# One hybrid mixer block on one core: the mixers' steps handed out in another order

## The chip, the cores and the metric

The kernel runs on 1 core of one Trainium2 chip. The metric is the device time of one execution in microseconds (us), the median of several runs. TensorE (PE in the profile) multiplies matrices and transposes, VectorE (DVE) and ScalarE (ACT) do the elementwise work, GpSimd (POOL) a few small operations, and SyncE (SP) issues most of the transfers. Each engine works through its own queue of instructions in order.

## What is computed

The reference is one block with a latent stream `x` of 1024 tokens by 1024 channels and a context of 256 tokens. One input projection feeds four mixers of 256 channels each, their outputs are joined and projected back, and a feed-forward part follows:

```python
y_a, yc_a = mlstm_mixer(z[..., :OFF_B], zc_a, ...)           # bidirectional chunkwise mLSTM
y_b = sgu_mixer(z[..., OFF_B:OFF_C], ...)                    # spatial gating, chunks of 128
y_c = conv_mixer(z[..., OFF_C:OFF_D], ...)                   # 31 taps, LayerNorm, SiLU
y_d, yc_d = s5_mixer(z[..., OFF_D:], zc_d, ...)              # bidirectional S5
y = jnp.concatenate([y_a, y_b, y_c, y_d], axis=-1) @ w_out[l]
x = layer_norm(ALPHA * x + g1 * y, ln1_w[l], ln1_b[l])
x = layer_norm(ALPHA * x + g2 * swiglu(x * (1.0 + sc2) + sh2, w_ffn_in[l], w_ffn_out[l]), ln2_w[l], ln2_b[l])
```

`g1`, `sh2`, `sc2` and `g2` are parts of the modulation `silu(c) @ w_mod + b_mod`, which is 6 times 1024 columns wide.

## The kernel before

Large products are three passes over values split in a high and a low half (`split2`: the high half on ACT, L831, the low on DVE, L832). Weights come in pieces of 512 KB through two `raw` buffers on SP's queue and are split into `whl` or `pg` tiles. `projT` (L861) makes a projection with channels on the partitions, `projK` (L870) with tokens on them. A projection `latT` writes its result with an activation (L1084).

Two forces set the order. The code says in which order steps are handed to a list scheduler: what comes first in the code goes first, and a later step fills in where an earlier one is not ready. Buffers and PSUM banks then hold a step back until an earlier user has let go. PSUM has three banks `mm` for the projections, two `a`, two `b` and one `c`. Bank `c` is shared by the modulation (L1010), the gating's mixing (L611, L647) and both transposes of the convolution's norm (L691, L700).

The steps of the mixers, and the lines to which they go:

- mLSTM (`y["a"]`): `mlstm_gates` (L370 to L474), `mlstm_states` (L478 to L525: the recurrent states `mC` of all eight chunks, a chain of small steps), then `mlstm_chunk` for each of 8 chunks of 128 tokens. A chunk has PE make the scores in bank `a` (L536) and, for each of two directions, the decay exponents in bank `b` (L543, L544, L546). ACT takes the exponential into `mD` (L549), DVE multiplies the scores on (L553), PE makes the states' part (L559) and the chunk's own part (L568), and DVE puts them together (L563 to L579). `mlstm_norm` takes two chunks at a time (L589 to L603).
- Gating (`y["b"]`): two projections `u` and `v`, the latter into `gv` (L870 and L1142), constants of the mixing weights (L611), and for each half of the tokens a norm (L636) and the mixing (`sgu_mix`: PE L647 into bank `c`, DVE L650 and L653).
- Convolution (`y["c"]`, in place in `ap`): `conv_taps` for each of two blocks of channels (50 DVE operations each, L673 to L681), and `conv_norm` for each of four quarters of the tokens (PE L691 into `c`, DVE L623 to L627, ACT L625 and L696, PE L700 into `c` again, and ACT's SiLU L702).
- Modulation: six late groups of 512 columns (`mod_late`). A group loads 8 pieces of 256 KB (`mw`, in two buffers) on SP's queue. DVE adds each onto the one buffer `macc` (L997, L999), PE sums over the partitions (L1010), and DVE adds the offsets (L1011). The first two groups make `g1`, spread over a tile by PE at L1151; the third is half of `sh2`.

`out_proj(0)` follows. For a half of the tokens it splits the four mixers' outputs (ACT L1198, DVE L1199), loads `x` (L1202) and multiplies by `w_out` (L1211), eight row blocks in the order d, b, c, a:

```python
KORD = (6, 7, 2, 3, 4, 5, 0, 1)
```

Three of its tiles stand in the three `mm` banks at a time, with 24 matmuls each: 6 with d, 6 with b, 6 with c, 6 with a. L1215 and L1216 add the result to `x`; `ln1` norms it (L1231 transposes it for the feed-forward part).

ACT holds the tables of one set of functions at a time: exponential (L549), square root (L625) and SiLU (L702) each bring a row `ACT_TABLE_LOAD` when the set before was another.

In the words of the new order's table, the code before hands out: `ctx_k ctx_v conv_in.0 conv_in.1 conv_w val gates key states query chunk.0 chunk.1 chunk.2 chunk.3 out_gate norm.0 norm.2 mod.0 mod.1 mod.2 sgu_u sgu_v gate1 sgu_w sgu.0 taps.0 taps.1 conv_n.0 conv_n.1 chunk.4 chunk.5 chunk.6 chunk.7 norm.4 norm.6 sgu.1 conv_n.2 conv_n.3`.

Of the kernel before, what the change touches and what calls it, by code (L numbers as in the profile page):

```python
# [705 lines left out]
D = 1024  # L706
# [54 lines left out]
    return np.ascontiguousarray(np.concatenate([c[n] for n, _ in CST], 1))  # L761


def body(tc, A, out):
# [5 lines left out]
    with st:  # L770
# [272 lines left out]
        Wk = [wtile(A["wk"][kh], 4, 256) for kh in range(2)]
        for j in range(2):
            ps = ps_mm()
            projK(Wk, ctxl(j), ps[:, 0:256])
            a.activation(kxc[:, j], ps[:, 0:256], AF.Copy, scale=0.125)
        Wv = wvg()
        for j in range(2):
            ps = ps_mm()  # L1050
            projK(Wv, ctxl(j), ps[:, 0:272])
            evac_vg(ps, vxc[:, j], j)
# [14 lines left out]
        wc = mx.tile([128, 2, 31], F32, name="wc")  # L1067
        gp.dma_start(wc, A["conv_t"])
        tc.keep_in_program_order(v.tensor_scalar(wc, wc, 0.5, None, op0=MUL))
        wcs = mx.tile([128, 2, 16], F32, name="wcs")  # L1070
        conv_sums(e, wc, wcs)

        vx = mx.tile([128, 8, 4, 65], F32, name="vx", tag="vx")
        Wv = wvg()
        for j in range(8):
            ps = ps_mm()
            projK(Wv, lat(j), ps[:, 0:272])
            evac_vg(ps, vx[:, j], 2 + j)
# [17 lines left out]
        kT = latT(page([128, 2, 1024]), "k", AF.Copy, scale=0.125)
        C = mp.tile([128, 8, 2, 2, 65], F32, name="mC", tag="mC")
        mlstm_states(e, G, kxc, vxc, kT, vx, C, mp)
        qT = latT(page2([128, 2, 1024]), "q", AF.Copy)
        y["c"] = ap.rearrange("p j r t -> p j (r t)")[:, :, 0:D]  # L1100
        hb = C.rearrange("p c r d x -> p c (r d) x")[:, :, :, 0:64]

        def chunks(hf):
            for c in range(hf * 4, hf * 4 + 4):
                mlstm_chunk(e, G, c, qT, kT, vx[:, c], hb[:, c], mp)

        def norms(hf):
            for c in range(hf * 4, hf * 4 + 4, 2):
                mlstm_norm(e, hb[:, c:c + 2], mp.tile([128, 8, 64], F32, name="msq", tag="mD", bufs=3), c, col["mnw"],
                           y["a"], y["a"], mp, NC=2)  # L1110

        def mlstm_half(hf):
            chunks(hf)
            norms(hf)

        def conv_half(hf):
            for q in range(hf * 2, hf * 2 + 2):
                conv_norm(e, ap, y["c"], q, col["clw"], col["clb"], mx)
# [16 lines left out]
        y["b"] = latT(page2([128, 2, 1024]), "u", AF.Gelu_apprx_tanh)  # L1135
        gv = page2([128, 8, 256])
        Wb = [wtile(A["wb"][kh], 4, 256) for kh in range(2)]
        for j2 in range(4):
            ps = ps_mm()
            for i in range(2):  # L1140
                projK(Wb, lat(j2 * 2 + i), ps[:, i * 256:(i + 1) * 256])
            a.activation(gv[:, j2 * 2:j2 * 2 + 2].rearrange("p i x -> p (i x)"), ps, AF.Gelu_apprx_tanh)  # L1142

        g1d = page([128, 2, D])
        g1 = g1d[:, 1]
        for i in range(8):
            v.tensor_scalar(g1d[:, 0, i * 128:(i + 1) * 128], e.ident, m2c[:, i:i + 1], None, op0=MUL)
        for c in range(2):
            cs_ = slice(c * 512, (c + 1) * 512)
            ps = ps_mm()  # L1150
            pe.matmul(ps, lhsT=bc(e.one, [128, 128]), rhs=g1d[:, 0, cs_], start=True, stop=True)  # L1151
            a.copy(g1[:, cs_], ps)
        wsT, bsb = mp.tile([128, 4, 128], F32, name="gw"), mp.tile([128, 2, 128], F32, name="gbs", tag="mC0")
        gp.dma_start(wsT, A["sgu_wt"])
        gp.dma_start(bsb, A["sgu_bb"])
        B = bsb
        sgu_consts(e, col["glb"], bsb, wsT, B)
# [442 lines left out]
```

## Time and profile before

| | us |
|---|---|
| median of 3 runs (lowest, highest) | 1175.17 (1174.21, 1177.67) |
| the profiled execution | 1174.72 |
| its span, first to last instruction | 1172.9 |
| PE busy | 1130.4 |
| DVE busy | 915.1 |
| ACT busy | 477.3 |
| mean granted clock of PE, full speed as 1 | 0.982 |

A row of the profile gives the engine, the line of the code, the operation, the tile written and the tiles read (`out<-in`), and a count. The chain of waits runs back from the last instruction, at each step to what released it. A row of the timeline has start, duration, instruction, and in brackets the idle time before it with what ended it. A matmul on 32-bit floats that are not split (L536, L559, L568, L611, L647, L691, L1010) counts as two records in the trace and one in an order listing. `PEclk` is the clock granted to PE.

### The profile page before, as it was taken

How to read it: one execution, taken by the hardware profiler on the slowest of the kernel's cores; microseconds unless marked ns; L12 is line 12 of the kernel's file. 1: busy time of each engine (PE TensorE's matmuls, PEld its weight loads, DVE VectorE, ACT ScalarE, POOL GpSimd, SP SyncE). 2: the span in 40 equal slices, each digit the busy share in tenths (PEclk: the TensorE clock that was granted, in tenths of full speed). 3: DMA queues.
4: the chain of work that ended last, by engine and by line, in shares of the span. 5: the costliest groups of instructions: out<-in, count | busy, mean ns of one | idle time of the engine just before them, and what ended most of it. 6: DMA issues, size and time to landing. Idle time of an engine off the chain costs nothing.

```text
span 1172.9 us, 15466 instructions
## 1 busy us (share of the span) xinstructions
PE 1130.4 (96%) x5763; PEld 909.8 (78%) x5763; DVE 915.1 (78%) x1751; ACT 477.3 (41%) x746; POOL 10.6 (1%) x33
## 2 busy tenths in 40 slices
PE   7989999999999899999999999999999989999996
PEld 4777788668897687768887888888887778888884
DVE  7778899988996699879868677776778767766775
ACT  4735444412428464582233332333232336433431
POOL 0010000000000000000000000000000000000000
PEclk8999999999999799999999999999999999999998
DMA  9652101121233165452233544435444789766621
GB/s 349 233 176 75 49 24 52 45 86 37 81 118 125 55 203 193 114 209 79 101 138 113 180 182 177 152 135 202 178 169 170 270 269 321 242 200 214 195 101 72
DMA packets 68316, 178.41 MB, mean 152 GB/s; under 512 B 7761, under 2 KB 15089, under 8 KB 66834
## 3 DMA queue, kind: packets, MB, share of 16 engines
q1 hardware_dynamic: 67826, 176.45, 43.8%
q0 software_dynamic: 272, 0.70, 0.3%
q8 instruction: 45, 0.74, 0.3%
q10 hardware_dynamic: 144, 0.29, 0.1%
q14 instruction: 29, 0.24, 0.1%
HBM read 136.80 MB, written 40.62 MB: 151 GB/s over the span
## 4 chain that ended last, share of the span: by engine, by line
PE 72%; DVE 14%; DMA 6%; ACT 5%; issue 2%; DVEq 0%; SPq 0%; ACTq 0%
PE mm L1372 16%; PE mm L861 11%; PE a L1372 8%; PE mm L1497 5%; PE mm L1211 4%; PE b L1372 4%; PE b L861 4%; PE a L1497 3%; PE b L1497 3%; PE mm L870 2%; PE c L1497 2%; DVE whl L832 2%; DVE pg L832 1%; PE b L568 1%; DMA mw<-in_w_mod_dram 1%
## 5 line engine op out<-in xcount | busy, mean ns | idle before, releaser
L861 PE MATMUL mm<-pg,whl 128*128 128x512 f32 x792 | 218.2, 410 | 1.9 <-ACT pg L1234 1.2
L831 ACT CAST whl<-raw 128x512 fp32r<-128x512 f32 (+1 forms) x198 | 119.6, 621 | 238.0 <-PE mm L1372 51.2
L1372 PE MATMUL mm<-pg,whl 128*128 128x512 f32 x864 | 206.0, 390 | 0.4 <-DVE whl L832 0.3
L1372 PEld LDWEIGHTS mm<-pg,whl 128*128 128x128 f32 x864 | 161.9, 188 | 35.6 <-issue 0.7
L861 PEld LDWEIGHTS mm<-pg,whl 128*128 128x128 f32 x792 | 144.2, 192 | 36.9 <-issue 5.6
L832 DVE TENSOR_TENSOR whl<-raw,whl 128x512 fp32r<-128x512 f32 (+1 forms) x198 | 133.1, 689 | 50.0 <-ACT whl L831 48.1
L1372 PE MATMUL a<-pg,whl 128*128 128x512 f32 x432 | 104.7, 390 | 3.7 <-ACT whl L831 3.7
L1372 PEld LDWEIGHTS a<-pg,whl 128*128 128x128 f32 x432 | 80.7, 188 | 21.4 <-ACT whl L831 4.9
L832 DVE TENSOR_TENSOR pg<-raw,pg 128x1024 fp32r<-128x1024 f32 (+1 forms) x52 | 59.6, 1150 | 23.3 <-ACT pg L831 23.2
L832 DVE TENSOR_TENSOR pg<-whl,pg 128x1024 fp32r<-128x1024 f32 (+1 forms) x42 | 47.4, 1133 | 32.4 <-ACT pg L831 28.4
L831 ACT CAST pg<-raw 128x1024 fp32r<-128x1024 f32 (+1 forms) x52 | 51.5, 991 | 50.4 <-DMA raw<-in_w_dram 18.7
L831 ACT CAST pg<-whl 128x1024 fp32r<-128x1024 f32 (+1 forms) x42 | 41.1, 980 | 66.4 <-PE c L1497 25.4
L870 PE MATMUL mm<-whl,pg 128*128 128x256 f32 (+1 forms) x448 | 64.9, 292 | 0.7 <-ACT whl L831 0.7
L870 PEld LDWEIGHTS mm<-whl,pg 128*128 128x128 f32 x448 | 59.3, 193 | 3.2 <-issue 1.7
L1372 PE MATMUL b<-pg,whl 128*128 128x512 f32 x216 | 51.9, 389 | 0.0
L1211 PE MATMUL mm<-whl,pg 128*128 128x512 f32 x192 | 49.9, 397 | 1.0 <-DVE pg L1199 1.0
L1211 PE MATMUL mm<-pg 128*128 128x512 f32 x192 | 49.5, 399 | 0.0
L1497 PE MATMUL mm<-pg,pg 128*128 128x512 f32 x171 | 48.0, 389 | 0.0
L1497 PE MATMUL a<-pg,pg 128*128 128x512 f32 x162 | 47.2, 390 | 0.3 <-DVE hs L1511 0.3
L1497 PE MATMUL b<-pg,pg 128*128 128x512 f32 x162 | 47.1, 389 | 0.0
L1372 PEld LDWEIGHTS b<-pg,whl 128*128 128x128 f32 x216 | 40.5, 188 | 8.4
L1211 PEld LDWEIGHTS mm<-whl,pg 128*128 128x128 f32 x192 | 35.3, 188 | 9.3 <-DVE pg L1199 1.8
(473 smaller groups left out, 1880.8 us busy)
## 6 DMA issues: line engine op xcount, KB each, us to landing
raw<-in_w_dram SPq DMA_DIRECT2D x59, 512.0 KB
gd<-pg SPq DMA_DIRECT2D x22, 1024.0 KB
whl<-gd SPq DMA_DIRECT2D x35, 512.0 KB
pg<-in_w2k_dram SPq DMA_DIRECT2D x11, 1024.0 KB
td<-pg SPq DMA_DIRECT2D x11, 1024.0 KB
raw<-td SPq DMA_DIRECT2D x20, 512.0 KB
raw<-in_wo_dram SPq DMA_DIRECT2D x16, 512.0 KB
raw<-in_wt_dram SPq DMA_DIRECT2D x14, 512.0 KB
```

What stands on the lines that cost most here:

```text
L568: pe.matmul(ps[:, x * 65:(x + 1) * 65], lhsT=D[d][:, x], rhs=vx[:, h, :], start=True, stop=True)
L831: a.copy(hi, r)
L832: v.tensor_tensor(lo, r, hi.bitcast(F32), op=SUB)
L861: pe.matmul(ps[h], lhsT=W(wi, k), rhs=rhs(hi, h, k), **f)
L870: pe.matmul(ps, lhsT=lhs(hi, k), rhs=Ws[k // 4](wi, k % 4), start=(k == 0 and n == 0), stop=(k == 7 and n == 2))
L1211: pe.matmul(ps, lhsT=Yr(hi, half, k)[:, t * 128:(t + 1) * 128], rhs=Ws[k // 2](wi, k % 2), start=(i + n == 0), stop=(i == 7 and n == 2))
L1372: pe.matmul(ps, lhsT=W[:, wi, k, :], rhs=B[b][hi][:, k], start=(first and k + n == 0), stop=(k == 3 and n == 2), skip_group_check=True)
L1497: pe.matmul(ps[t], lhsT=Ag[:, hi, k, t * 128:(t + 1) * 128], rhs=Bg[:, wi, k], start=(first and k0 + k + m == 0), stop=(k0 + k == NK - 1 a ...
```

## The change

The block of the mixers, from the context's projections to the mixers' last norms, is cut into named steps. Each step has the same instructions as before. A string gives the order in which they are handed to the scheduler. `sgu.1`, `conv_n.2` and `conv_n.3`, which stood just ahead of `out_proj(0)`, are among them.

```diff
+ORDER = """ctx_v ctx_k conv_in.1 conv_in.0 conv_w val gates key taps.0 states query chunk.3 taps.1 out_gate chunk.0 mod.2 chunk.2
+conv_n.0 chunk.1 sgu_u norm.2 mod.0 mod.1 norm.0 sgu_v gate1 sgu_w sgu.0 chunk.7 chunk.4 chunk.6 conv_n.1 chunk.5 conv_n.2
+norm.4 norm.6 sgu.1 conv_n.3"""
...
+        @do
+        def states():
+            C = mp.tile([128, 8, 2, 2, 65], F32, name="mC", tag="mC")
+            mlstm_states(e, X.G, kxc, vxc, X.kT, X.vx, C, mp)
+            X.hb = C.rearrange("p c r d x -> p c (r d) x")[:, :, :, 0:64]
...
+        def chunk(c):
+            mlstm_chunk(e, X.G, c, X.qT, X.kT, X.vx[:, c], X.hb[:, c], mp)
...
+        def mod(i):
+            mod_late(range(i, i + 1), lambda: mx.tile([128, 512], F32, name="macc", tag="kxc"),
+                     lambda: mx.tile([128, 512], F32, name="mw", tag=("vxc", "mw")[next(mq) % 2]), "c")
...
+        def conv_n(q):
+            conv_norm(e, ap, y["c"], q, col["clw"], col["clb"], mx)
+
+        def run(order):
+            for n in order.split():
+                if n in step:
+                    step[n]()
+                else:
+                    f, i = n.rsplit(".", 1)
+                    dict(conv_in=conv_in, chunk=chunk, norm=norm, mod=mod, sgu=sgu_half, taps=taps, conv_n=conv_n)[f](int(i))
+
+        run(ORDER)
...
-        chunks(0)
-        y["a"] = latT(page2([128, 2, 1024]), "o", AF.Sigmoid)
-        norms(0)
-        mq = iter(range(99))
-        mod_late(range(0, 3), lambda: mx.tile([128, 512], F32, name="macc", tag="kxc"),
-                 lambda: mx.tile([128, 512], F32, name="mw", tag=("vxc", "mw")[next(mq) % 2]), "c")
...
-        sgu_half(0)
-        taps(0)
-        taps(1)
-        conv_half(0)
-        mlstm_half(1)
...
-        sgu_half(1)
-        conv_half(1)
         out_proj(0)
```

In the new file the lines below 764 keep their numbers; L831 and L861 become L836 and L866, L870 becomes L875, L1010 becomes L1015, L1198 becomes L1245, and L1211 becomes L1258.

**ACT, the second half's chunks.** First the program of before, where ACT serves chunks 4 to 7 (exponentials into `mD`) and the convolution's first two norms (`cmv`, `cxn`, `ap`):

```order
L549 ACT_TABLE_LOAD
L549 ACTIVATE mD<-b 128x512
L625 ACT_TABLE_LOAD
L625 ACTIVATE cmv<-cmv,oz 128x2
L696 ACTIVATE cxn<-c,cmv 128x256 x2
L549 ACT_TABLE_LOAD
L549 ACTIVATE mD<-b 128x512
L702 ACT_TABLE_LOAD
L702 ACTIVATE ap<-c,cols 128x256 x2
L549 ACT_TABLE_LOAD
L549 ACTIVATE mD<-b 128x512
L1198 CAST pg<-ap 128x1024
```

The same place in the changed program, up to the split of the same `ap`:

```order
L625 ACT_TABLE_LOAD
L625 ACTIVATE cmv<-cmv,oz 128x2
L549 ACT_TABLE_LOAD
L549 ACTIVATE mD<-b 128x512
L836 CAST pg<-raw 128x1024
L549 ACTIVATE mD<-b 128x512
L696 ACTIVATE cxn<-c,cmv 128x256 x2
L549 ACTIVATE mD<-b 128x512 x2
L702 ACT_TABLE_LOAD
L702 ACTIVATE ap<-c,cols 128x256 x2
L1245 CAST pg<-ap 128x1024
```

The exponentials now stand together, and one SiLU (of quarter 1) instead of two stands in this place; quarter 0's norm is done earlier.

**PE, the same place.** Before, from the last matmuls with b to the first with c (`mm<-pg` alone, without `whl`); `gw` is the gating's mixing weight, `cst` the identity, `cr` the constants of the decay:

```order
L700 MATMUL c<-cst,cxn 128x128 x4
L568 MATMUL b<-vx,mD 128x65 x4
L647 MATMUL c<-gw,pg_3292 64x128 x11
L559 MATMUL a<-mC,pg_2600 128x130 x4
L568 MATMUL b<-vx,mD 128x65 x4
L536 MATMUL a<-pg_2600,pg 128x128 x4
L647 MATMUL c<-gw,pg_3292 64x128 x5
L1211 MATMUL mm<-pg 128x512 x3
```

And in the changed program, again up to the first matmuls with c. Ahead of these rows stand three transposes L700, three matmuls L1258 with b and four L568:

```order
L1258 MATMUL mm<-whl,pg 128x512
L559 MATMUL a<-mC,pg_2652 128x130 x4
L568 MATMUL b<-vx,mD 128x65 x4
L536 MATMUL a<-pg_2652,pg 128x128 x4
L543 MATMUL b<-cr 128x512
L544 MATMUL b<-mR_2264,cr 128x512
L546 MATMUL b<-cr,mAL_2263 128x512
L543 MATMUL b<-cr 128x512
L544 MATMUL b<-mR_2275,cr 128x512
L546 MATMUL b<-cr,mAL_2274 128x512
L691 MATMUL c<-cst,ap 64x128 x8
L1258 MATMUL mm<-pg 128x512 x18
```

The mixing L647 of the second half has left this place. The last matmul with b now stands one chunk ahead of those with c, which follow 18 in a row.

**PE, the modulation.** Before, the three late groups lie in the projections of the gate and of the gating, one after the other:

```order
L1010 MATMUL c<-oz,macc 128x1 x4
L861 MATMUL mm<-pg,whl 128x512 x8
L600 MATMUL b<-cst,msq 128x128 x4
L861 MATMUL mm<-pg,whl 128x512 x13
L870 MATMUL mm<-whl,pg 128x256 x79
L1010 MATMUL c<-oz,macc 128x1 x4
L870 MATMUL mm<-whl,pg 128x256 x113
L1151 MATMUL mm<-pg,oz 128x512 x2
```

These are the second and the third group. In the changed program the second and third handed out (`mod.0`, `mod.1`) stand thus:

```order
L1015 MATMUL c<-oz,macc 128x1 x4
L875 MATMUL mm<-whl,pg 128x256 x50
L600 MATMUL b<-cst,msq 128x128 x4
L875 MATMUL mm<-whl,pg 128x256 x59
L1015 MATMUL c<-oz,macc 128x1 x4
L875 MATMUL mm<-whl,pg 128x256 x7
L600 MATMUL b<-cst,msq 128x128 x4
L875 MATMUL mm<-whl,pg 128x256 x34
L1180 MATMUL mm<-pg,oz 128x512 x2
```

The last group now stands 41 instead of 113 of the `v` projection's matmuls ahead of `g1`'s (L1151, now L1180), and `macc` must be full there.

More of the change, by code (lines that the diff above doesn't have):

```diff
@@ L1040, in body, with do, ctx_k, ctx_v @@
         s5.release()
[L1043 to L1052, printed above, removed]
+        step = {}
+        def do(f):
+            step[f.__name__] = f
+            return f
+        X = Env()
+        @do
+        def ctx_k():
+            Wk = [wtile(A["wk"][kh], 4, 256) for kh in range(2)]
+            for j in range(2):
+                ps = ps_mm()
+                projK(Wk, ctxl(j), ps[:, 0:256])
+                a.activation(kxc[:, j], ps[:, 0:256], AF.Copy, scale=0.125)
+        @do
+        def ctx_v():
+            Wv = wvg()
+            for j in range(2):
+                ps = ps_mm()
+                projK(Wv, ctxl(j), ps[:, 0:272])
+                evac_vg(ps, vxc[:, j], j)
         ap = mx.tile([128, 2, 16, 96], F32, name="ap", tag="ap")
         gp.memset(ap, 0.0)
-        for j in range(2):
+        y["c"] = ap.rearrange("p j r t -> p j (r t)")[:, :, 0:D]
+        def conv_in(j):
             ps, _ = projT(wtile(wT["ca"][j], 8, 128), (0, 1), Hr)
@@ L1066, in body, with conv_w, val @@
                     v.scalar_tensor_tensor(w_, th, 1.0, w_, op0=ADD, op1=MUL)
[L1067 to L1078, printed above, removed]
+        @do
+        def conv_w():
+            X.wc = mx.tile([128, 2, 31], F32, name="wc")
+            gp.dma_start(X.wc, A["conv_t"])
+            tc.keep_in_program_order(v.tensor_scalar(X.wc, X.wc, 0.5, None, op0=MUL))
+            X.wcs = mx.tile([128, 2, 16], F32, name="wcs")
+            conv_sums(e, X.wc, X.wcs)
+        @do
+        def val():
+            X.vx = mx.tile([128, 8, 4, 65], F32, name="vx", tag="vx")
+            Wv = wvg()
+            for j in range(8):
+                ps = ps_mm()
+                projK(Wv, lat(j), ps[:, 0:272])
+                evac_vg(ps, X.vx[:, j], 2 + j)
         def latT(o, name, func, **kw_):
@@ L1096, in body @@
[L1096 to L1118, printed above, removed]
+        @do
+        def gates():
+            cr = mp.tile([128, 434], F32R, name="cr")
+            v.tensor_copy(cr[:, 0:128], e.ident)
+            v.tensor_copy(cr[:, 128:434], cst[:, off["sel1"].start:off["maskb"].stop])
+            e.identr, e.sel1, e.sel2 = cr[:, 0:128], cr[:, 128:138], cr[:, 138:178]
+            e.mask = cr[:, 178:434].rearrange("p (d t) -> p d t", d=2)
+            X.G = mlstm_gates(e, Gk, mp.tile([128, 2080], F32, name="mC", tag="mC"), mp)
@@ new lines, in key, with query, out_gate @@
+        @do
+        def key():
+            X.kT = latT(page([128, 2, 1024]), "k", AF.Copy, scale=0.125)
+        @do
+        def states():
+            C = mp.tile([128, 8, 2, 2, 65], F32, name="mC", tag="mC")
+            mlstm_states(e, X.G, kxc, vxc, X.kT, X.vx, C, mp)
+            X.hb = C.rearrange("p c r d x -> p c (r d) x")[:, :, :, 0:64]
+        @do
+        def query():
+            X.qT = latT(page2([128, 2, 1024]), "q", AF.Copy)
+        @do
+        def out_gate():
+            y["a"] = latT(page2([128, 2, 1024]), "o", AF.Sigmoid)
@@ new lines, in chunk, with norm @@
+        def chunk(c):
+            mlstm_chunk(e, X.G, c, X.qT, X.kT, X.vx[:, c], X.hb[:, c], mp)
+        def norm(c):
+            mlstm_norm(e, X.hb[:, c:c + 2], mp.tile([128, 8, 64], F32, name="msq", tag="mD", bufs=3), c, col["mnw"],
+                       y["a"], y["a"], mp, NC=2)
+        mq = iter(range(99))
+        def mod(i):
+            mod_late(range(i, i + 1), lambda: mx.tile([128, 512], F32, name="macc", tag="kxc"),
+                     lambda: mx.tile([128, 512], F32, name="mw", tag=("vxc", "mw")[next(mq) % 2]), "c")
@@ new lines, in sgu_u, with sgu_v @@
+        @do
+        def sgu_u():
+            y["b"] = latT(page2([128, 2, 1024]), "u", AF.Gelu_apprx_tanh)
+        @do
+        def sgu_v():
+            X.gv = page2([128, 8, 256])
+            Wb = [wtile(A["wb"][kh], 4, 256) for kh in range(2)]
+            for j2 in range(4):
+                ps = ps_mm()
+                for i in range(2):
+                    projK(Wb, lat(j2 * 2 + i), ps[:, i * 256:(i + 1) * 256])
+                a.activation(X.gv[:, j2 * 2:j2 * 2 + 2].rearrange("p i x -> p (i x)"), ps, AF.Gelu_apprx_tanh)
@@ new lines, in gate1 @@
+        @do
+        def gate1():
+            g1d = page([128, 2, D])
+            X.g1 = g1d[:, 1]
+            for i in range(8):
+                v.tensor_scalar(g1d[:, 0, i * 128:(i + 1) * 128], e.ident, m2c[:, i:i + 1], None, op0=MUL)
+            for c in range(2):
+                cs_ = slice(c * 512, (c + 1) * 512)
+                ps = ps_mm()
+                pe.matmul(ps, lhsT=bc(e.one, [128, 128]), rhs=g1d[:, 0, cs_], start=True, stop=True)
+                a.copy(X.g1[:, cs_], ps)
@@ L1135, in body @@
[L1135 to L1157, printed above, removed]
-        sgu_half(0)
```

22 lines of the change are left out of this document (11 added, 11 removed).

## The prediction, made before the run

> **What bounds the kernel now.** I read the page's shares and its chain first, then a table of stretches, then the chain and the timelines in the stretch that stands out.
>
> ```profile
> PE 1130.4 (96%) x5763; PEld 909.8 (78%) x5763; DVE 915.1 (78%) x1751; ACT 477.3 (41%) x746; POOL 10.6 (1%) x33
> PE 72%; DVE 14%; DMA 6%; ACT 5%; issue 2%; DVEq 0%; SPq 0%; ACTq 0%
> ```
>
> PE is busy for 96% of the span, and the change takes no matmul away. So it can gain only where PE waits, or where PE is busy at less than its full clock. The change touches the mixers up to `out_proj(0)`. Its stretches in the trace of before (columns: window, length, then busy time and count of PE, PEld, DVE, ACT, POOL, granted clock, DMA share, GB/s):
>
> ```profile
> 204.65:357.39 152.74, 150.80 (x920) 119.40 (x921) 132.29 (x311) 53.83 (x90) 3.40 (x8) 1.00 0.22 70
> 357.39:381.50 24.11, 24.11 (x178) 17.61 (x176) 17.76 (x45) 20.02 (x29) 0.00 (x0) 1.00 0.43 153
> 381.50:400.43 18.93, 15.03 (x99) 12.22 (x98) 11.60 (x32) 10.64 (x13) 0.00 (x0) 0.73 0.01 1
> 400.43:410.76 10.33, 10.33 (x62) 8.30 (x62) 6.85 (x19) 2.53 (x4) 0.00 (x0) 0.83 0.40 154
> 410.76:460.00 49.24, 48.29 (x237) 39.09 (x237) 46.51 (x89) 26.88 (x37) 0.00 (x0) 1.00 0.65 212
> ```
>
> I call the first row A (from the last S5 products to `g1`'s L1151), the next three B (the second half's chunks beside the start of `out_proj(0)`), the last C (the rest of it). Within B the third row stands out: PE idles for 3.9 us and has a clock of 0.73. No matmul L1211 stands in it. The 36 matmuls with d and b of three tiles are through, and the part with c waits for the convolution's first two quarters. The chain shows why it lasts (start, duration, what):
>
> ```profile
> 385.55 0.90 ACT cxn L696 x2
> 386.45 0.13 issue
> 386.58 1.28 ACT L549
> 387.86 0.01 issue
> 387.87 0.60 ACT mD L549
> 388.47 0.02 issue
> 388.49 1.28 ACT L702
> 389.77 0.01 issue
> 389.78 1.03 ACT ap L702 x2
> ...
> 390.86 2.00 PE c L647 x16
> ...
> 393.68 1.11 PE c L647 x6
> ...
> 400.50 1.58 PE mm L1211 x3
> ```
>
> ACT is asked for two tables by turns: exponentials for the chunk and SiLU for the convolution, 1.28 us for each load. Then PE, thinly fed, gets half its clock:
>
> ```profile
> 386.00:390.00 4.00, 2.28 (x16) 1.83 (x14) 3.35 (x8) 3.94 (x6) 0.00 (x0) 1.00 0.00 0
> 390.00:392.00 2.00, 1.50 (x16) 1.36 (x16) 0.00 (x0) 1.98 (x3) 0.00 (x0) 0.60 0.04 8
> 396.00:400.00 4.00, 4.00 (x25) 3.66 (x26) 2.56 (x5) 0.91 (x1) 0.00 (x0) 0.50 0.00 0
> 400.00:404.00 4.00, 4.00 (x12) 2.93 (x10) 3.50 (x7) 0.73 (x2) 0.00 (x0) 0.50 0.50 181
> ```
>
> **What the hole is worth.** The same matmuls at full clock, from places of before where PE was dense:
>
> ```profile
> 289.70 0.72 PE L559 MATMUL a<-mC,pg 64*128 64x130 f32 x8
> 290.36 1.11 PE L568 MATMUL b<-vx,mD 128*128 128x65 f32 x8
> 291.39 0.72 PE L536 MATMUL a<-pg,pg 64*128 64x128 f32 x8
> 386.93 0.60 PE L700 MATMUL c<-cst,cxn 128*128 128x128 f32 x4
> 360.87 1.09 PE L647 MATMUL c<-gw,pg 128*64 128x128 f32 x16
> ```
>
> From start to next start a group of eight L559 takes 0.66, eight L568 take 1.03 (289.70, 290.36, 291.39). I take 0.66 for eight L536 too, 0.60 for the L700 and 1.09 for sixteen L647. The six decay matmuls of a chunk take 1.4 (an estimate: six at the 0.23 of a 512-wide matmul, row below). The hole holds sixteen L559 (1.3), twenty-four L568 (3.1), sixteen L536 (1.3), the decay matmuls of one chunk (1.4), L700 (0.6) and thirty-two L647 (2.2): 9.9 us of work in 18.93. So 9.0 us are lost there, and behind it PE runs at half clock from 400.43 to about 404, which loses 1.8 more. **The hole costs 10.8 us.**
>
> **Part by part.** The norms of quarters 0 and 1, the chunks' order and the moved mixing meet in the hole. Quarter 0's norm is handed out ahead of `sgu_u` and its SiLU is done long before. Quarter 1's L691 no longer competes with `sgu.1` for the one bank `c`, since its L647 now comes behind the chunks. From the decay matmuls of chunk 6 on, ACT has to do two exponentials (1.2), one table load (1.28), two SiLU (1.03) and the cast, and DVE the split (row below), before the first matmul with c: 1.2 + 1.28 + 1.03 + 1.05 + 1.22 = 5.8 us.
>
> ```profile
> 597.94 2.72 PE mm L1372 x12
> 343.91 13.65 PE mm L870 x113
> L1198 ACT CAST pg<-pg 128x1024 fp32r<-128x1024 f32 x4 | 4.1, 1047 | 0.0
> L1199 DVE TENSOR_TENSOR pg<-ap,pg 128x1024 fp32r<-128x1024 f32 x1 | 1.2, 1216 | 0.0
> ```
>
> PE's own rows between these points in the new order are three L700 (0.45), three matmuls with b at 2.72 / 12 = 0.227 (0.7), eight L568 in the trace's count (1.03), one with b (0.2), eight L559 (0.66), eight L568 (1.03), eight L536 (0.66), the decay matmuls of chunk 5 (1.4) and the sixteen L691, taken at the 1.09 of sixteen L647. That is 7.2, more than 5.8, so c is ready when PE comes to it and the hole closes. The cover is thin, 1.4 us. A small wait for L568 on its `mD` is likely: I keep **+1.0**, from 0 up to +4.5, half of what the waits and clock take in the hole now.
>
> The clock goes with the hole: at 386 to 390 PE was busy 2.28 of 4 us, and where PE is dense in the table the clock is 1.00.
>
> *Taps, chunks and norms in A.* DVE carries A nearly as densely as PE: 132.29 of 152.74. Taps now come ahead of the states and two chunks early. I laid the new order on the durations of before. At the first two chunks handed out (3 and 0) DVE's work up to the product L553 is 1.2 us more than PE's up to the matmul that needs it, an estimate from the group means; at chunks 2 and 1 there is about 1 us to spare. A delay shifts PE as a whole, so the second costs nothing if the first was paid: **+1.0**. At best A's present idle time goes (152.74 - 150.80 = 1.94, so -1.9); at worst both waits are paid and a table load stands ahead of one of them (2.4 + 1.28 = +3.7).
>
> *The modulation.* A group asks for 8 loads of 256 KB in two buffers and one `macc`, and the next can't begin to add until L1010 has read `macc`.
>
> ```profile
> 308.12 0.79 PE c L1010 x8
> ...
> 326.33 0.95 PE L1010 MATMUL c<-oz,macc 128*128 128x1 f32 x8
> 342.88 1.02 PE L1010 MATMUL c<-oz,macc 128*128 128x1 f32 x8 [0.74 <-DVE macc L997]
> 332.40 2.85 DMA mw<-in_w_mod_dram
> 336.12 4.79 DMA mw<-in_w_mod_dram
> ```
>
> Two L1010 are 16.55 us apart in before, and PE waited 0.74 at the second. In the new order PE has 109 of the L870 (13.65 / 113 = 0.121 each, 13.2 together), L1010 (0.8) and L600 (about 0.5) between the last two: 14.5. At the same pace PE waits 2.05, that is 1.3 more than now: **+1.3**. At best the wait is gone (-0.7); at worst the pace is that of the first two groups, 18.2 from 308.12 to 326.33, or +3.0. Each of these loads stands in SP's queue, and the second half of the `v` projection's weights stands behind some of them; that is a rival below.
>
> *C.* `sgu.1` and the last two norms now lie beside `out_proj(0)`. PE's own work is the same as it was elsewhere. DVE, busy 46.51 of 49.24, gets the gating's norm and mixing (about 2.9 us), and DVE also has to empty the `mm` banks (L1215). **+0.5**: from -0.9 (C's idle, 49.24 - 48.29) to +2.9.
>
> The one table load less in all, and four fewer in B, are on ACT, which was busy 41% of the span; outside the hole PE hides them.
>
> **Sum:** -10.8 + 1.0 + 1.0 + 1.3 + 0.5 = -7.0 us. Against the profiled execution, 1174.72, that is 1167.7. The median of the runs is 0.45 above it, so I say **1168.2**. With every bound at its best the change is -10.8 - 1.9 - 0.7 - 0.9 = -14.3, at its worst +3.3.
>
> **Rivals.**
>
> *The half clock comes anyway* (0.11). New thin places arise in A or with the last norms, and the clock falls there. In before it lasted some 13.6 us (0.60 in 390 to 392 means from about 390.4, and until 404); on dense PE half of that is 6.8. Then -7.0 + 6.8 = -0.2, or 1175.0. For it: gaps of 1.7 us at most were enough. Against it: A and C ran at 1.00 with DVE as dense as it will be.
>
> The Trainium skill, page "TensorE: Matmul & The Clock Gate", section "Part 1: The HAM clock gate", says that the clock halves after an idle window of about 3.4 us and comes back after about 3.4 us of sustained work. The rows above differ on both: the clock fell after 4 us in which PE was busy 2.28, and it stayed at 0.50 through 8 us with PE busy 4.00 of 4. By the page's figure a new fall would cost half of 3.4, 1.7 us, an estimate, and the sum with it would be -5.3; I go by the rows.
>
> *The hole stays by half* (0.14). Quarter 1's statistics are DVE and ACT work (L623 to L627, L625 with its own table load) that queue behind chunk products. If they come 5 us late, c is late again and some 4.5 us stay: -2.5, or 1172.7. For it: the cover of 1.4 us. Against it: the new order puts these statistics ahead of chunk 4's exponentials on ACT.
>
> *The modulation's loads become the bound: slower* (0.12). Between the L1010 of `mod.2` and `g1`'s L1151 the new order has 192 of the L870 (23.2), 27 matmuls of the `u` projection (6.1), and small rows of two chunks, of `conv_n.0` and of the groups, by the rows above about 12: some 41 us of PE's work. Two of the 16 loads can be there beforehand; 14 remain, so PE begins to wait at 41 / 14 = 2.9 us a load, and the whole gain is eaten at (41 + 8.3) / 14 = 3.5. Before, the pace was 16.55 / 8 = 2.07, with two under way at a time; single loads took 2.85 and 4.79. In the new order they share SP's queue with the `u` and `v` weights, and each is held until DVE has added an earlier one. If they came one by one, at the mean of those two, 3.82, `g1` would be 14 x 3.82 - 41 = 12.5 late. With the 1.3 above replaced, the sum is -7.0 - 1.3 + 12.5 = +4.2: 1179.4. Against it: the two buffers made 2.07 of those.
>
> *Better than the sum* (0.07). The waits in A go too, and all closes: about -12, or 1163.2.
>
> That the change doesn't do what it says is excluded by the order shown: the steps do move.
>
> **How the numbers follow.** The forecast case (-4 to -11) has 0.56. Time moves that a measurement can tell start at about 0.3%, 3.5 us. Faster takes the forecast, the better case and a little under half of the halved hole, which straddles that line: 0.56 + 0.07 + 0.06 = 0.69. Within 0.3% are the rest of it and the half clock: 0.08 + 0.11 = 0.19. Slower is the loads: 0.12. The range runs from 1161.5 (near the best of every bound) to 1175.5, which takes in both rivals that end near no change and leaves out the slower one and the rest of the tail.
>
> **What would show it.** Right: no stretch without `out_proj` matmuls between the last with b and the first with c, a clock of 1.00 through the second half's chunks, and the first L1231 (the transposes of `ln1`) some 7 us earlier against the S5 part. The step on A is wrong if PE's idle time between S5 and L1180 grows by more than 4 us; the modulation's if L1015 or L1180 waits for DMA or for `macc` more than 3 us; the one on C if PE waits for DVE at L1215's banks. The prediction as a whole is wrong if another half-clock stretch of over 10 us appears, or if the c part still waits for L1246 (L1199 of before).

## The result, and the profile after

| | before | after |
|---|---|---|
| median of 20 runs each, us | 1173.57 | 1164.79 |
| ratio of the runs, 95% interval | | 0.993 (0.9913 to 0.9946) |
| profiled execution, us | 1174.72 | 1162.93 |
| its span, us | 1172.9 | 1161.2 |
| its mean granted clock | 0.982 | 0.989 |

The changed kernel is 0.5 to 0.9% faster, some 8 us. The forecast was -7.0 and 1168.2, with a range of 1161.5 to 1175.5. One run on each side, 5770.54 before and 2067.6 after, stood far off; the ratio leaves them out, and without them the medians are 1172.93 and 1164.71. The two profiled executions lie 11.8 apart, more than the medians: the one of before lies 1.2 above its median, the one of after 1.9 below.

Two rows of the profile's page after, in the same order as before:

```profile
PE 1123.4 (97%) x5763; PEld 903.3 (78%) x5763; DVE 913.6 (79%) x1751; ACT 475.1 (41%) x745; POOL 10.6 (1%) x33
PE 75%; DVE 13%; DMA 4%; ACT 4%; issue 3%; SPq 1%; DVEq 0%; POOL 0%; ACTq 0%
```

PE does the same 5763 matmuls in 7.0 us less of busy time. Shorter busy time for the same rows fits a clock that fell less (0.989 for 0.982); the order alone can change it too, as e6 shows below. The stretches of the changed kernel, with the columns of before (the last S5 products to `g1`; to the last matmul with b; to the first with c; to the last L568; to the first transpose of `ln1`):

```profile
203.35:358.57 155.22, 152.53 (x938) 119.69 (x939) 135.08 (x319) 62.26 (x100) 3.35 (x8) 1.00 0.22 69
358.57:386.10 27.53, 27.53 (x200) 21.33 (x198) 22.12 (x58) 18.40 (x28) 0.00 (x0) 1.00 0.40 135
386.10:391.40 5.30, 5.30 (x49) 4.06 (x48) 4.05 (x8) 4.77 (x7) 0.00 (x0) 1.00 0.00 0
391.40:398.60 7.20, 7.20 (x46) 6.14 (x45) 5.68 (x17) 2.58 (x4) 0.00 (x0) 1.00 0.24 74
398.60:482.66 84.06, 83.42 (x417) 67.92 (x417) 78.14 (x160) 39.23 (x56) 0.00 (x0) 1.00 0.55 177
```

The third row is what was the hole: 5.30 us instead of 18.93, PE busy all the time, clock 1.00. The first row is 2.5 us longer than before. The timelines of PE, ACT and DVE show why nothing waits between b and c:

```profile
384.24 0.49 PE L700 MATMUL c<-cst,cxn 128*128 128x128 f32 x3
384.48 0.94 PE L1258 MATMUL mm<-whl,pg 128*128 128x512 f32 x3
385.26 1.00 PE L568 MATMUL b<-vx,mD 128*128 128x65 f32 x8
...
390.38 1.09 PE L691 MATMUL c<-cst,ap 128*64 128x128 f32 x16
391.40 0.96 PE L1258 MATMUL mm<-pg 128*128 128x512 f32 x3
```

```profile
383.79 1.29 ACT L549 ACTIVATE mD<-b 128x512 f32<-128x512 f32 x2 [6.39 <-issue]
385.10 1.28 ACT L702 ACT_TABLE_LOAD   x1
386.40 1.02 ACT L702 ACTIVATE ap<-c,cols 128x256 f32<-128x256 f32 x2
387.45 1.05 ACT L1245 CAST pg<-ap 128x1024 fp32r<-128x1024 f32 x1
```

```profile
388.69 1.22 DVE L1246 TENSOR_TENSOR pg<-ap,pg 128x1024 fp32r<-128x1024 f32 x1
```

The two exponentials stand together, one table load follows, and the split's cast ends at 388.5. DVE's part of the split ends at 389.9, so c is there 1.5 us before PE has done with the chunk and with L691 at 391.4. No row of PE has an idle time in brackets.

### The profile page after: what moved, and what is told of

It reads as the page before. It is cut to its first block, busy times and chain, and to the rows that moved or that the text cites. A ratio compares the mean times of both kernels' runs of the same rounds, so it can differ in the third digit from the quotient of the medians.

```text
span 1161.2 us, 15445 instructions
## 1 busy us (share of the span) xinstructions
PE 1123.4 (97%) x5763; PEld 903.3 (78%) x5763; DVE 913.6 (79%) x1751; ACT 475.1 (41%) x745; POOL 10.6 (1%) x33
## 4 chain that ended last, share of the span: by engine, by line
PE 75%; DVE 13%; DMA 4%; ACT 4%; issue 3%; SPq 1%; DVEq 0%; POOL 0%; ACTq 0%
PE mm L1417 16%; PE mm L866 12%; PE a L1417 8%; PE mm L1258 5%; PE mm L1542 5%; PE b L1417 4%; PE b L866 4%; PE a L1542 3%; PE b L1542 3%; PE mm L875 2%; PE c L1542 2%; DVE pg L837 1%; PE b L568 1%; DVE whl L837 1%; DVE macc L1002 1%
## 5 line engine op out<-in xcount | busy, mean ns | idle before, releaser
L836 ACT CAST whl<-raw 128x512 fp32r<-128x512 f32 (+1 forms) x198 | 119.8, 622 | 259.4 <-PE mm L1417 50.5
L866 PE MATMUL mm<-pg,whl 128*128 128x512 f32 x792 | 216.2, 408 | 1.7 <-ACT pg L1281 1.3
L866 PEld LDWEIGHTS mm<-pg,whl 128*128 128x128 f32 x792 | 144.1, 191 | 37.5 <-issue 5.9
L836 ACT CAST pg<-raw 128x1024 fp32r<-128x1024 f32 (+1 forms) x52 | 51.4, 991 | 44.8 <-DMA raw<-in_w_dram 18.2
L836 ACT CAST pg<-whl 128x1024 fp32r<-128x1024 f32 (+1 forms) x42 | 41.1, 981 | 66.3 <-PE b L1542 25.4
L875 PE MATMUL mm<-whl,pg 128*128 128x272 f32 (+1 forms) x448 | 65.0, 290 | 0.0
L875 PEld LDWEIGHTS mm<-whl,pg 128*128 128x128 f32 x448 | 58.5, 190 | 2.3 <-issue 1.7
L1258 PE MATMUL mm<-whl,pg 128*128 128x512 f32 x192 | 49.0, 395 | 0.2 <-DVE pg L1246 0.2
L1258 PE MATMUL mm<-pg 128*128 128x512 f32 x192 | 48.1, 394 | 0.0
L1258 PEld LDWEIGHTS mm<-whl,pg 128*128 128x128 f32 x192 | 35.5, 188 | 8.2 <-DVE pg L1246 0.7
```

The source lines that it names most:

```text
L836: a.copy(hi, r)
L866: pe.matmul(ps[h], lhsT=W(wi, k), rhs=rhs(hi, h, k), **f)
L875: pe.matmul(ps, lhsT=lhs(hi, k), rhs=Ws[k // 4](wi, k % 4), start=(k == 0 and n == 0), stop=(k == 7 and n == 2))
L1258: pe.matmul(ps, lhsT=Yr(hi, half, k)[:, t * 128:(t + 1) * 128], rhs=Ws[k // 2](wi, k % 2), start=(i + n == 0), stop=(i == 7 and n == 2))
```

## The experiments

All twelve use the changed kernel's code with another order string, or the order of before with a few more transposes. The order of before in this code gives PE the rows of the kernel before. The table gives, for one profiled execution of each, the time between starts on PE: from the first L338 to `g1`'s first matmul, from there to the first matmul of `out_proj` with c, and from there to `ln1`'s first transpose. Then come the median time, the ratio to before with its interval, and the median clock of the runs. Each ratio is to the runs of before that stood beside that experiment: 18 beside e1 to e4, 31 beside e5 to e8, 25 beside e9 to e12, with medians of 1173.97, 1174.91 and 1173.78. The clock given for before is that of these 74 runs.

| run | S5 to g1 | g1 to c (PE idle) | c to ln1 | median us | ratio | clock |
|---|---|---|---|---|---|---|
| before | 152.7 | 43.0 (3.9) | 93.8 | 1173.57 | | 0.983 |
| after | 155.2 | 32.8 (0.0) | 91.3 | 1164.79 | 0.993 (0.9913 to 0.9946) | 0.991 |
| e1 first new, second old | 157.4 | 28.3 (0.4) | 100.2 | 1168.39 | 0.994 (0.9915 to 0.9965) | 0.990 |
| e2 first old, second new | 152.1 | 44.3 (3.7) | 89.6 | 1170.18 | 0.9974 (0.9945 to 1.0003) | 0.988 |
| e3 taps ahead only | 159.7 | 41.5 (2.8) | 99.9 | 1183.27 | 1.0074 (1.0053 to 1.0094) | 0.982 |
| e4 taps and norm back | 150.3 | 41.1 (2.3) | 89.2 | 1165.94 | 0.9955 (0.9924 to 0.9986) | 0.988 |
| e5 before, wait filled | 152.5 | 39.3 (3.0) | 91.3 | 1168.83 | 0.9955 (0.993 to 0.9979) | 0.989 |
| e6 early norm back | 153.8 | 42.1 (2.6) | 90.7 | 1169.37 | 0.9963 (0.9941 to 0.9985) | 0.990 |
| e7 third group late | 155.1 | 34.5 (0.1) | 91.5 | 1165.12 | 0.9939 (0.9914 to 0.9965) | 0.989 |
| e8 taps between | 151.2 | 43.1 (3.7) | 92.5 | 1171.48 | 0.9985 (0.9958 to 1.0011) | 0.984 |
| e9 both norms first | 150.5 | 37.0 (2.8) | 96.7 | 1172.70 | 0.9991 (0.9968 to 1.0014) | 0.985 |
| e10 e9 with old start | 150.3 | 33.0 (1.2) | 93.3 | 1160.93 | 0.9889 (0.9837 to 0.9941) | 0.991 |
| e11 new with old start | 157.2 | 34.3 (0.0) | 91.9 | 1167.08 | 0.9943 (0.9918 to 0.9968) | 0.991 |
| e12 before, filled elsewhere | 153.0 | 44.6 (2.0) | 93.2 | 1176.78 | 1.002 (0.9983 to 1.0057) | 0.982 |

The middle stretches don't hold the same work everywhere. Quarter 0's norm (16 L691 in the trace's count and 4 L700, the 16 at 1.02 and 4 at 0.11 each, some 1.5 us of PE, by the rows of after's chain below) stands ahead of `g1` in after, e1, e7, e8 and e11, behind it in the others. The first stretch of one and the same order repeats within 0.5 us (before, e12 and e5: 152.7, 153.0, 152.5). Between the first L338 and `ln1` the clock was at 0.50 for 13.7 us in before, 6.8 in e1 and in e2, 23.9 in e3, 3.4 in e6, 13.7 in e8 and 20.5 in e12; in the other profiles it was not.

```profile
384.40 0.33 PE c L700 x3
...
390.45 1.02 PE c L691 x16
391.47 3.62 PE mm L1258 x15
```

**Which part closes the hole: e1 to e4.** Theory 1 was that quarter 0's early norm does it, theory 2 that the second half's order does.

```diff
-sgu.0 chunk.7 chunk.4 chunk.6 conv_n.1 chunk.5 conv_n.2 norm.4 norm.6 sgu.1 conv_n.3
+sgu.0 conv_n.1 chunk.4 chunk.5 chunk.6 chunk.7 norm.4 norm.6 sgu.1 conv_n.2 conv_n.3
```

> The new order up to sgu.0 (taps ahead, quarter 0's convolution norm ahead of the u projection), then the second half in the old order: conv_n.1, chunks 4 5 6 7, norms, sgu.1, conv_n.2, conv_n.3. Theory 1 (quarter 0's early norm closes the hole: only one norm and one SiLU are left between the matmuls with b and those with c): 8 to 10 us under before, no half clock in the second half's chunks, PE idle in the stretch from g1 to the last L568 under 1 us. Theory 2 (the second half's new order of chunks and norms closes it, since the exponentials stand together): the hole stays, 0 to 3 us over before.

The hole is gone, so theory 2 falls as the only cause. But the time is only 0.6% under before. The first stretch is 157.4 in the profile, some 1.7 of it from a half clock of 3.4 us there (356.2 to 359.6), and behind c PE waits for the next half's split.

```profile
PE mm L1256 <- DVE pg L1244: 1.8, 1, 1.8
```

This row is of e1's table of waits (what waited, for what, us in all, times, longest); L1244 is the low half's split in `out_proj`. In after, which differs from e1 in the second half's order alone, the same wait is 0.2 us.

```diff
-chunk.0 chunk.1 chunk.2 chunk.3 ... sgu.0 taps.0 taps.1 conv_n.0 conv_n.1 chunk.4 chunk.5 chunk.6 chunk.7 norm.4 norm.6 sgu.1 conv_n.2 conv_n.3
+chunk.0 chunk.1 chunk.2 chunk.3 ... sgu.0 taps.0 taps.1 conv_n.0 chunk.7 chunk.4 chunk.6 conv_n.1 chunk.5 conv_n.2 norm.4 norm.6 sgu.1 conv_n.3
```

> The old order up to conv_n.0 (taps and quarter 0's norm behind sgu.0), then the second half in the new order (chunks 7 4 6, conv_n.1, 5, conv_n.2, norms, sgu.1, conv_n.3). Theory 1 (the early norm does it): 13 us of chunk rows stand between the last matmul with b and the first with c, the hole stays with waits of some 5 to 9 us, the time is within 3 us of before. Theory 2 (the order of chunks does it): 8 to 10 us under before, with no wait over 1 us there.

The waits stay, as theory 1 expects, but they are 3.7 us and not 5 to 9. The time is a little under before, within what the interval leaves open.

```diff
-key states ... chunk.0 chunk.1 ... mod.2 sgu_u ... sgu.0 taps.0 taps.1 conv_n.0 conv_n.1
+key taps.0 states ... chunk.0 taps.1 chunk.1 ... mod.2 conv_n.0 sgu_u ... sgu.0 conv_n.1
```

> The old order with only the two blocks of taps and quarter 0's norm in their new places (taps.0 ahead of the states, taps.1 behind chunk 0, conv_n.0 ahead of sgu_u). Theory 1 (the early norm closes the hole): 7 to 10 us under before, the hole shrinks to the waits of one chunk, the clock stays at 1.00 there. Theory 2 (the order of chunks): within 3 us of before, hole and half clock as they were.

Both theories miss the time: 9 us over before. But this run doesn't test an early norm. Though handed out ahead of `sgu_u`, quarter 0's norm has its first L691 at 368.55, behind the third late group in bank `c` (367.27) and behind `g1`'s first matmul (365.75); in after it stands at 316.79. With the old order of the rest, early taps lengthen the first stretch by 7.0 us, and quarter 1's SiLU is still late. A row of PE's waits in e3:

```profile
PE c L647 <- ACT ap L702: 1.3, 1, 1.3
```

PE was busy 1.95 of 4 us at that place, and the clock was 0.50 for the 16 us behind it:

```profile
396.00:400.00 4.00, 1.95 (x22) 1.57 (x22) 2.38 (x6) 3.96 (x7) 0.00 (x0) 0.86 0.47 135
400.00:404.00 4.00, 4.00 (x22) 2.91 (x22) 2.24 (x4) 0.48 (x1) 0.00 (x0) 0.50 0.00 0
...
412.00:416.00 4.00, 4.00 (x17) 2.82 (x16) 0.93 (x2) 1.40 (x3) 0.00 (x0) 0.50 0.38 131
```

So e3 shows what early taps cost in the old order, and nothing of an early norm; e6 below tests that one.

```diff
-key taps.0 states query chunk.3 taps.1 out_gate chunk.0 mod.2 chunk.2 conv_n.0 chunk.1 ... sgu.0 chunk.7
+key states query chunk.3 out_gate chunk.0 mod.2 chunk.2 chunk.1 ... sgu.0 taps.0 taps.1 conv_n.0 chunk.7
```

> The new order with both blocks of taps and quarter 0's norm back behind sgu.0, everything else new. Theory 1: the hole is back, within 4 us of before. Theory 2: 8 to 10 us under before. Both: PE's idle time before g1's matmuls is smaller than in the changed kernel by up to 1 us, since DVE is not asked for the taps ahead of the first chunks.

The hole is back with 2.3 us of waits, as theory 1 says, but its time fails: it is near that of the changed kernel. Part of that is A, 4.9 shorter than in after, of which the norm is only 1.5; the rest, 3.4, is more than the waits. In the profiled execution, at 1163.41, the clock stays at 1.00 through the hole. Over ten runs the times go with the clock: five at 0.990 and above took 1163.1 to 1164.9, three at 0.986 and 0.987 took 1167.0 to 1171.7, two at 0.981 and 0.982 took 1174.0 and 1176.1. So with the same order and its waits, the executions with a low clock take some 10 us more. That made a third theory: the half clock is most of what the hole costs.

**The clock: e5 and e12.** e5 fills the longest wait of the hole with useless work; e12 does the same work where PE is dense.

```diff
 # conv_norm (e5)
-    for j in range(2):
+    for j in [0, 1] * (3 if q == 1 else 1):
         for i in range(2):
             pe.transpose(ps[:, (j * 2 + i) * 128:(j * 2 + i + 1) * 128], xn[:, i, j * 128:(j + 1) * 128], e.ident)
```

> The order of before, with the four transposes of quarter 1's convolution norm (L700) done three times over instead of once; the rest of each engine's order is that of before. The 8 more stand in the wait of 1.72 us ahead of L568 in the hole and add about 1 us of PE work there, so PE is busy some 3.2 of 4 us instead of 2.28. Theory clock (the thin feed brings the half clock, and the half clock is a good part of the hole): the clock stays at 1.00 from 386 to 404, 3 to 6 us under before in spite of the added work. Theory waits (ACT's and DVE's chain holds the hole, the clock costs little): the time within 1.5 us of before, whatever the clock does.

```diff
 # ln1 (e12)
-                for i in range(4):
+                for i in list(range(4)) * (3 if half == 1 and k == 4 else 1):
```

> The order of before with 8 more transposes of the same size where PE is dense (the fifth group of ln1's transposes in the second half done three times), as a control to the filled wait. Theory clock: PE does 1 us more work and the hole with its half clock is as in before, so 0 to 2 us over before, clock about 0.98. Rival (the filled wait gained for another reason, such as any added matmuls): 3 us or more under before.

The timeline and the windows of e5:

```profile
385.77 1.47 PE L700 MATMUL c<-cst,cxn 128*128 128x128 f32 x12
388.10 1.11 PE L568 MATMUL b<-vx,mD 128*128 128x65 f32 x8 [0.85 <-DVE mD L553]
```

```profile
384.00:388.00 4.00, 3.25 (x26) 2.60 (x22) 3.76 (x12) 3.57 (x5) 0.00 (x0) 1.00 0.02 6
388.00:392.00 4.00, 2.55 (x29) 2.17 (x30) 1.53 (x5) 3.96 (x6) 0.00 (x0) 1.00 0.00 0
392.00:396.00 4.00, 4.00 (x40) 3.30 (x38) 3.57 (x9) 1.53 (x2) 0.00 (x0) 1.00 0.00 0
```

The wait ahead of L568 is 0.85 instead of 1.72, the clock stays at 1.00, and with 8 transposes more the program is 0.5% faster than before. All ten runs had clocks of 0.986 to 0.992. The control e12 gains nothing. Nine of its ten runs had clocks of 0.978 to 0.984, and its profile has the half clock, from 384.1 to 404.5, sooner and longer than before, behind 4 us with PE busy 3.17:

```profile
380.00:384.00 4.00, 3.17 (x29) 2.38 (x26) 2.12 (x8) 2.57 (x4) 0.00 (x0) 1.00 0.24 95
...
386.00:390.00 4.00, 3.91 (x12) 2.70 (x10) 3.04 (x7) 2.80 (x5) 0.00 (x0) 0.50 0.01 2
...
398.00:402.00 4.00, 4.00 (x25) 3.33 (x25) 2.40 (x5) 1.04 (x1) 0.00 (x0) 0.50 0.00 0
402.00:406.00 4.00, 4.00 (x13) 3.07 (x13) 3.65 (x9) 1.14 (x2) 0.00 (x0) 0.68 0.76 253
```

The 74 runs of the kernel before that stood beside these experiments point the same way without any edit. Over them each 0.001 of mean clock went with 0.97 us (least squares, correlation -0.87): 38 runs at clocks up to 0.983 have a median of 1176.1, 11 runs from 0.987 up one of 1168.1. The mean clock counts every fall of an execution, not the hole's alone: the profile of before has three more, of 3.4 us each, outside the stretches of the table. By the mean clocks the kernel before has the long fall in most executions, not in all.

**What A pays: e6, e7 and e11.**

```diff
-chunk.2 conv_n.0 chunk.1 ... sgu.0 chunk.7
+chunk.2 chunk.1 ... sgu.0 conv_n.0 chunk.7
```

> The new order with only quarter 0's convolution norm back behind sgu.0; the taps stay ahead of the states and behind chunk 3. Theory 1 (the early norm closes the hole, the taps only make it possible and cost DVE time among the first chunks): the hole as in the run with taps and norm back (c part some 41 us behind g1's matmuls, 2 to 3 us idle), and the stretch from the last S5 products to g1's matmuls 152.5 to 154: 1166 to 1169, slower than both the changed kernel and the run with the taps back. Theory 3 (the early taps cost nothing, the norm's 1.6 us of PE work is all that A gains): that stretch 150 to 151.5, time 1163 to 1166.

With this one step back the hole is back, with 2.6 us of waits. So in the new order the early norm is needed to close it. In e1, e7 and e11, as in after, the norm stands ahead of `g1` and PE idles 0.4 us at most in the middle stretch; e8 is taken up below. In all runs with the norm behind `g1` PE idles 1.2 us or more there.

The first stretch is 153.8, 3.5 more than with the taps back (150.3); the early norm adds another 1.4 (155.2), its own work. Theory 1's sizes for A hold, theory 3 falls. But the early taps cost little in waits: PE's idle time in the stretch is 2.2 us in e6 and 2.3 in e4. More of the cost is in busy time: 32 L536 and 32 L559 keep PE busy for 4.7 and 3.6 us in e6, for 3.1 and 2.9 in e4. In e6 more of their groups of eight are split in two, and four take as long as eight. First e6, 0.64 us to the next start, then e4, 0.65:

```profile
300.05 0.71 PE L559 MATMUL a<-mC,pg 64*128 64x130 f32 x4
300.69 0.66 PE L568 MATMUL b<-vx,mD 128*128 128x65 f32 x4
```

```profile
298.09 0.72 PE L559 MATMUL a<-mC,pg 64*128 64x130 f32 x8
298.74 1.11 PE L568 MATMUL b<-vx,mD 128*128 128x65 f32 x8
```

The rest of the new first half makes the stretch 2.4 us shorter than before (152.7 to 150.3).

```diff
-chunk.0 mod.2 chunk.2 ... sgu.0 chunk.7
+chunk.0 chunk.2 ... sgu.0 mod.2 chunk.7
```

> The new order with the modulation group mod.2 (only needed by ln1) moved from between chunks 0 and 2 to behind sgu.0. Theory loads (16 loads behind mod.2's eight make PE wait at the third group's matmuls and DVE adds crowd the first chunks, 1 to 3 us in A): A 1.5 to 3 us shorter than in the changed kernel, 1161 to 1164. Rival (the adds only move, DVE is as dense behind g1, and the c part waits for it): A shorter by as much, the stretch behind it longer by as much, within 1.5 us of the changed kernel.

The theory of the loads falls: A is 155.1 instead of 155.2. The rival too expected a shorter A; only its time holds, 0.3 us from the changed kernel. In the changed kernel PE waits 0.67 us at the third group, about the 0.74 of before (rows of PE's timeline):

```profile
337.00 0.95 PE L1015 MATMUL c<-oz,macc 128*128 128x1 f32 x8
...
352.22 1.05 PE L1015 MATMUL c<-oz,macc 128*128 128x1 f32 x8 [0.67 <-DVE macc L1002]
```

```diff
-ctx_v ctx_k conv_in.1 conv_in.0
+ctx_k ctx_v conv_in.0 conv_in.1
```

> The new order with only the first four steps in the old order (ctx_k ctx_v conv_in.0 conv_in.1). Theory start: the 0.9 us wait at L407 goes and the stretch from S5 to g1 is about 154.5 instead of 155.3, the time 0.5 to 1.5 us under the changed kernel. Rival: within 0.7 us of the changed kernel.

The wait at L407 went, another of 0.6 us at L386 came, and A was 2.0 longer. The theory of the start falls.

**Better orders: e8 to e10.** They try to have the short first stretch without the hole.

```diff
-taps.0 states query chunk.3 taps.1 out_gate chunk.0 mod.2 chunk.2 conv_n.0 chunk.1 sgu_u norm.2 mod.0 mod.1 norm.0 sgu_v gate1 sgu_w sgu.0 chunk.7
+states query chunk.3 out_gate chunk.0 chunk.2 chunk.1 taps.0 taps.1 sgu_u norm.2 mod.0 mod.1 norm.0 conv_n.0 sgu_v gate1 sgu_w sgu.0 mod.2 chunk.7
```

> A middle order: taps.0 and taps.1 behind chunk 1 ahead of sgu_u, quarter 0's norm ahead of sgu_v, mod.2 behind sgu.0, the rest new. The order has the same rows from the last matmul with b to the first with c as the changed kernel (CT, three matmuls with b, one chunk). Theory 1 with the cost of early taps in A: hole closed as in the changed kernel and A 2 to 4 us shorter (151 to 153.5): 1159 to 1163, faster than the changed kernel. Rival (taps in the projections of u delay the modulation's adds, and L1010 waits instead): A 154 to 157, 1163 to 1167.

A is 151.2 with the norm in it, as hoped, and the matmuls with c follow those with b. But a new thin place came right behind `g1`, where PE waited 2.76 us for L553, and the half clock with it (a row of the timeline, and windows):

```profile
366.11 1.06 PE L568 MATMUL b<-vx,mD 128*128 128x65 f32 x4 [2.76 <-DVE mD L553]
```

```profile
364.00:366.00 2.00, 0.00 (x0) 0.00 (x0) 1.63 (x4) 1.84 (x3) 0.00 (x0) 1.00 1.03 422
366.00:370.00 4.00, 3.89 (x20) 3.77 (x21) 2.83 (x9) 1.99 (x2) 0.00 (x0) 0.53 0.36 142
370.00:376.00 6.00, 6.00 (x35) 4.55 (x31) 2.23 (x5) 0.00 (x0) 0.00 (x0) 0.50 0.00 0
```

This is the first rival of the prediction, in another order.

```diff
-taps.0 states ... taps.1 out_gate ... conv_n.0 chunk.1 ... sgu.0 chunk.7 chunk.4 chunk.6 conv_n.1 chunk.5
+states ... out_gate ... chunk.1 ... sgu.0 taps.0 taps.1 conv_n.0 conv_n.1 chunk.7 chunk.4 chunk.6 chunk.5
```

> The new order, but with the taps behind sgu.0 as in before, then the norms of quarters 0 and 1 both ahead of the second half's chunks 7 4 6 5. By the runs so far late taps make the first stretch (S5 to g1) 150.3 instead of 155.3 us, and the hole is held by quarter 1's SiLU. If both norms are handed out first, one chunk and three matmuls with b stand between the quarter's transposes and the first matmul with c, as in the changed kernel. Theory 1 (the hole closes whenever the norms are done a chunk before c is wanted; early taps are only one way to it): S5 to g1 150 to 151, g1 to the c part 35 to 37, clock at 1.00 there: 1159 to 1163. Theory 4 (taps behind sgu.0 are too late for both norms, DVE holds them): g1 to the c part 40 us or more, with waits over 2 us, 1164 to 1168.

In the profile the first two stretches come as theory 1 says, 150.5 and 37.0 (upper end), but the one behind is 5.4 longer than in after, with waits for the split again (2.1 us on L1244), and the thin place stays. The profiled execution, at 1167.74, kept its clock there:

```profile
385.00:390.00 5.00, 2.31 (x26) 1.86 (x25) 2.02 (x6) 4.94 (x7) 0.00 (x0) 1.00 0.01 3
```

The other nine runs had clocks of 0.980 to 0.986 and took 1171.5 to 1175.2. A profile that shows 1.00 at a thin place is one throw, not the rule.

> The run before this one with the first four steps in the old order (ctx_k ctx_v conv_in.0 conv_in.1). The wait of 0.9 us of PE for DVE at L407 in the gates, seen with the new start and not with the old, should go. Theory start (that wait is real and not made up later): about 1 us under the run with the new start, first stretch 149.5 to 150.5. Rival (other engines take it back): no difference over 0.7 us.

This is the fastest of all, 1160.93, all four runs at clocks from 0.991. But its expected cause fails: A is the same with either start (150.3 and 150.5). The gain stands in the other two stretches, 33.0 and 93.3. There the scheduler put other rows: five matmuls with b stand in place of three, and PE's waits before c are 1.2 us instead of 2.8. How the start brings this about was not followed up. By the medians it is 4 us under the changed kernel; the two intervals of the ratios overlap, so that it beats the changed kernel isn't shown.

## Why the prediction was right

*The hole* (-10.8, with +1.0 for what stays). Right in mechanism: with quarter 0's norm early it closes, with that norm back it does not (e6), and the rows between b and c came as laid out, 7.16 us of PE (384.24 to 391.40) for 7.2 and a cover of 1.5 for 1.4. In size it gave more than the sum said. From `g1` to `ln1` the time fell from 136.8 to 124.1, 12.7 less; 1.5 of it is quarter 0's norm, which moved to A and which the sum had left out on both sides. That leaves -11.2, against -9.3 with the term for C. What stayed of the hole was 0 instead of 1.0. Whether an early norm alone would do, in the order of before, was not tested.

*The clock.* The step said that it goes with the hole, and in the changed kernel's profile it did; e4 and e9 show a hole with the clock kept. Its remark that the clock is 1.00 where PE is dense misses its own row from 400.43, with PE busy throughout and a clock of 0.83: a fall outlasts the thin place. What the sum did not show is how much of its 10.8 the clock is. PE idled 3.9 us in the hole. The windows of before show the other part: busy time times the missing clock is 1.5 x 0.4 + (3.15 + 4 + 4) x 0.5 = 6.2 us from 390 to 404 (the row from 392 to 396 is the one line not shown with the prediction). e5 gained 5.3 us by its ratio (2.5 to 8.2 by the interval), and did 1 us more work; in its profile `g1` to `ln1` is 6.2 shorter than before (136.8 to 130.6). So the clock is the larger part, and the changed kernel's median of 1164.8 against 1168.1 for the runs of before with the highest mean clocks puts the rest, net of what A costs, at some 3 us, an estimate across separate runs.

```profile
392.00:396.00 4.00, 3.15 (x23) 2.18 (x19) 2.02 (x5) 1.63 (x3) 0.00 (x0) 0.50 0.00 0
```

*Taps, chunks and norms in A* (+1.0) *and the modulation* (+1.3). The sum, +2.3, is near, but by luck: A grew by 2.5, of which 1.5 is the moved norm, which the sum left out, and 1.0 loss. The single terms were mis-sized and cancel. Early taps cost 3.5 (e6 against e4), and for the most part not in the waits for L553 that the step named. The modulation's wait was 0.67 for 0.74, no change, where 2.05 was expected: the last group's matmuls were 15.2 us behind the second's (337.00 to 352.22), so its adds kept a faster pace than the 16.55 on which the term rested. The rest of the first half gave back 2.4, which no term had.

*C* (+0.5). From c to `ln1` 93.8 became 91.3, with 1.8 expected from the clock. The rest, -0.7 with ten matmuls more than before in the trace's count (462 for 452), lies on the other side of +0.5 and is too small to be tested.

*The rivals.* The loads as the bound did not come: 0.67 us at L1015 and none at L1180. In the one profile of the changed kernel the half clock does not come between S5 and `ln1` (behind it there are two falls of 3.4 us, as in before), but e8 and e3 show that its price and its place were real. A hole stayed in e4, e6 and e9; what it cost hung on the clock.

*The number.* -7.0 was forecast; the medians moved by -8.8, or -8.2 without the two far runs, and the profiles by -10.2 from S5 to `ln1`. Of the 11.8 between the profiled executions 1.4 stand ahead of S5, where the first L338 starts anywhere from 203.3 to 206.9 in the 14 profiles. How close the medians come to -7.0 is in part luck: it hangs on how many of the runs of before have the long fall. And the range was wide, before's own median lies in it.

Why the half clock comes in some executions and not in others of one program isn't settled. The Trainium skill, page "TensorE: Matmul & The Clock Gate", section "Part 1: The HAM clock gate", says that the window in which activity is counted runs freely, so the moment of a change varies from run to run. The spread of e4's ten runs and that of before agree with that. Its figure of about 3.4 us for the way back does not fit e8 and e3, where PE was busy all the time and the clock was 0.50 for 10 us and more; it fits e6, where in two windows of 4 us (0.11 x 4 + 0.31 x 4) / 0.5 = 3.4 us were at half clock (the other falls are in the last section):

```profile
396.00:400.00 4.00, 2.88 (x23) 2.69 (x23) 4.00 (x12) 3.60 (x5) 0.00 (x0) 0.89 0.42 131
400.00:404.00 4.00, 4.00 (x15) 3.31 (x15) 2.15 (x8) 2.30 (x3) 0.00 (x0) 0.69 0.90 312
```

## What to carry to other kernels

Where PE is 96% busy, look for stretches in which it is fed thinly for some 4 us and read the granted clock behind them: the clock there can cost more than the waits. Time many executions beside the profile, since at such a place one execution keeps its clock and the next doesn't. And test an order as a whole: here the same early taps were part of a gain of 9 us and, in the old order, of a loss of 9.
